# A two-layer hybrid decoder trunk on one core: new order of the first stage, its first transfers, the clears of the gated attention's tiles, and one operation at the end

## The chip, the cores and the metric

The kernel runs on one core of a Trainium2 chip. Its time is the device time of one execution in microseconds (us); the runs of a kernel give a median. A profile is of one execution, and has a time of its own. Engines: PE is TensorE (the matrix products), DVE is VectorE, ACT is ScalarE, POOL is GpSimd, SP is SyncE, which here only issues DMAs.

## What is computed

Two layers over x of 1024 tokens by 1024, in float32. The start of each layer, which the change is about, and its end:

```
c_act = silu(c)
mod = c_act @ w_mod + b_mod                      # 1024 -> 3*1024
shift, scale, gate = split(mod)
h = rms_norm(x, pre_gain) * (1.0 + scale) + shift
proj = h @ w_in                                  # to the heads of A, B, C and their gates
...
y = concat([a_out, r_out, g_out]) @ w_out
x = x + gate * rms_norm(y, post_gain)
```

A is sliding-window attention with rotary positions, B retention, C gated linear attention; each is multiplied by the silu of its own part of proj (gg is C's gate, rg B's, ga the low-rank input of C's decay).

## The kernel before, in words

Every float32 product is made of three passes of a faster format: an operand is split into a high part (a copy that rounds) and a low part (what the copy left, by a subtraction), and PE adds high by high, high by low and low by high. So each weight and each piece of h costs a copy (`high`, or line 503 for weights, mostly on ACT) and a subtraction (lines 844, 854 and 510, on DVE or POOL) before PE can use it. Weights come by DMA in pieces of 256 KB into staging tiles `st`.

The order of the work is written by the program itself while it is built: later stages are jobs, run when a running estimate of PE's time (`clk`) has passed their due time; a table `L` of lags shifts these due times. The first stage is not made of jobs. `first_stage` runs a list of steps written out by hand, `ORDER_1`, and its transfers are issued by another, `ORDER_0`, on SP's queue. The instructions of each engine stand in the order in which the steps emit them, and each engine works through its own list in order, waiting by semaphores for the others.

What the first stage computes: the modulation of layer 0 (shift and gain of 1024 columns) from eight pieces `wm` of w_mod, 1 MB each, and at the same time the norm and modulation of the first four token tiles (x0 to x3, 512 KB each), then from these the first product with gg's weights. The letters of `ORDER_1`, with their lines:

- `w`, `x`, `g`, `r`: issue a transfer (wm piece, x tile, a piece of gg's or rg's weights); `G`, `R`: split such a piece (lines 503 and 510); `v`: split ga's part (lines 865, 866).
- `q`, `o`, `n`: squares of an x tile on ACT (line 810), its root (line 618 on DVE, the power of line 621 on POOL), the scaling (line 816).
- `S`: the sum of a wm piece with c_act on PE (16 matmuls), copied by ACT (line 792); `C`: turn its row into columns (four small matmuls) and add the rows b_mod and norm gain (lines 798, 800), which PE had to transpose first.
- `T`, `U`: transposition of x tiles on PE, for tokens 0 to 255 and 256 to 511; `M`, `N`: modulation (line 829 on DVE, line 827 on ACT) and high part (line 835 on DVE, 833 on ACT); `L`, `K`: low part (lines 844, 854).
- `P`, `Q`: product of modulated pieces with gg's weights on PE (6 and 12 matmuls of 128x272).
- `t`: next step of the rotary table (VectorE operations of 512 columns in lines 372 to 398, one table load and two sines on ACT, lines 393 and 394).
- `z`, `y`: one spin, a product of the identity with itself whose result is never read. Number behind a letter: which piece, or how often.

`GLO` says which pieces of gg's (AG) and rg's (AV) first weights have the low part made on POOL. Ahead of the lists stand the transfers of c, constants (`c_early`), the positions, the rows b_mod and norm gain, and ga's weights, the positions' transposition, eight spins, and the silu of c (line 768's tanh on ACT, lines 770 and 771).

After the first stage the function `gla_tiles` (line 935) clears two tiles of 128x2048 for each layer, which C's products use as operands with zeros in places; the next projection of the heads follows. The layer's end (line 1595 on) computes the last two token tiles in halves; `rstd2` (line 624) adds two partial sums of squares (line 626), scales them and adds the epsilon (line 618), and takes the power -0.5 on POOL (line 621).

Of the kernel before, what the change touches and what calls it, by code (L numbers as in the profile page):

```python
# [91 lines left out]
def trunk(ctx: ExitStack, tc: tile.TileContext, ins, cst, out):  # L92
# [160 lines left out]
    c_nat = small(8)  # L253
    nc.sync.dma_start(c_nat, c_in.rearrange("o (p k) -> p (o k)", p=P))
    early = cload("early", eng=A)
# [368 lines left out]
    def rstd2(ss):  # L624
        sst = small(1)
        V.tensor_tensor(sst, ss[:, 0:1], ss[:, 1:2], ALU.add)
        return rstd_of(sst, 1, 1.0 / D, EPS)
# [93 lines left out]
    def first_stage():  # L721
# [3 lines left out]
        rows = t1()[0:24, 0:P]  # L725
        A.dma_start(rows[0:16, :], b_mod[0:1, 0:2 * D].rearrange("o (k p) -> (o k) p", p=P))
        A.dma_start(rows[16:24, :], pre_g[0:1, :].rearrange("o (k p) -> (o k) p", p=P))
        w = place(PLACE[0]["gg"])
        low = t1()[:, 0:128].rearrange("p (k n) -> p k n", k=KT)
        A.dma_start(low, w_ga[0])  # L730
        xk = [gp.tile([P, D], F32, tag=f"kT{t}", name=nm("xk"), bufs=1) for t in range(2)]
# [35 lines left out]
        V.tensor_copy(posf, pr[:, 0:8])  # L767
        A.activation(th0, c_nat, AF.Tanh, scale=0.5)
        more(3)
        V.scalar_tensor_tensor(c_act, th0, 1.0, c_nat, ALU.add, ALU.mult)  # L770
# [164 lines left out]
    def gla_tiles():  # L935

        for b in range(2):
            z_ = mix_tile(F32).rearrange("p a k q -> p (a k q)")
            G.memset(z_, 0.0)
# [574 lines left out]
    def last_output(l, load_mix):  # L1514
# [57 lines left out]
        for p in range(PLAIN // 2, NP_):  # L1572
# [52 lines left out]
            summed(y, pm, s1, s[:, 0:1], 0, h0)  # L1625
            V.tensor_tensor(s[:, 0:1], s[:, 0:1], s[:, 1:2], ALU.add)
            pm = bank()
            prod(pm[:, h1], a22, "T4", c=h1)
            add(y[:, h1], pm[:, h1], s1[:, h1])
            A.activation(stage()[:, h1], y[:, h1], AF.Square, accum_out=s[:, 2:3])  # L1630
            r = rstd2(s[:, 0:3:2])
            V.tensor_tensor(y[:, h1], y[:, h1], gcol[0][:, h1], ALU.mult)
# [207 lines left out]

ORDER_0 = "g x0 x1 w0 w1 x2 w2 g w3 g x3 w4 w5 w6"
ORDER_1 = (
# [4 lines left out]
)  # L1847
GLO = {'AG': (1, 3, 2), 'AV': (2,)}
B2, B1, BS, BST, MMB, SMB, BMOD = 10, 8, 11, 5, 2, 3, 3
# [56 lines left out]
}  # L1906
L = {"fx": 0.0, "fx@1": 3.24, "tt6": 12.28, "sw1": 2.01, "ld1": 1.66, "ld2": 1.76, "ld1@1": 0, "ld2@1": 0.07, "swW00": 5.37, "swT1": 0.43, "swW11": 1.72, "swW10": 6.15, "tt1": 15.57, "tt2": 5.14, "tt3": 7.18, "tt4": 3.16, "rq1": 17.87, "pf3@2": 0.68, "pf3@3": 1.67, "pf4@2": 4.07, "pf4@3": 9.27, "pf5": 0, "mod1": 12.02, "mod2": 2.2, "mod3": 8.51, "mod4": 8.54, "mod5": 4.17, "mod6": 9.91, "pre1": 9.84, "kv1": 4.07, "kv2": 9.26, "aq1": 6.02, "aq7": 6.16, "ag1": 4.54, "aq2": 2.75, "aq6": 6.49, "aq3": 11.06, "aq4": 6.85, "aq5": 4.05, "hn1": 8.92, "hn2": 6.14, "gz1": 18.33, "gz2": 11.8, "gl1": 9.81, "gd3": 17.03, "gc1": 0.98, "gc2": 6.16, "gc3": 1.97, "gc4": 0.1, "gc6": 0.8, "gc5": 1.44, "rc1": 3.56, "rc2": 2.88, "rc3": 7.08, "rc4": 5.77, "fin1": 8.69, "lay1": 0.27, "gc4@1": 0, "mod2@1": 4.09, "mod3@1": 12.43, "mod5@1": 4.25, "mod6@1": 5.5, "pre1@1": 7.09, "kv1@1": 5.87, "kv2@1": 2.64, "aq1@1": 4.88, "aq7@1": 5.14, "ag1@1": 2.87, "aq2@1": 1.05, "aq6@1": 6.78, "aq3@1": 8.64, "aq4@1": 5.48, "aq5@1": 5.73, "hn1@1": 8.28, "hn2@1": 0.73, "gz1@1": 15.9, "gz2@1": 11.94, "gl1@1": 3.31, "gd3@1": 16.2, "gc1@1": 0.0, "gc2@1": 2.01, "gc3@1": 0.83, "gc6@1": 1.61, "gc5@1": 0.72, "rc1@1": 4.88, "rc2@1": 2.79, "rc3@1": 5.12, "rc4@1": 0.8, "fin1@1": 8.37, "lay1@1": 11.61, "mod4@1": 5.36, "mod1@1": 6.02}
CHUNK = 7
# [44 lines left out]
```

## Time and profile before

| what | us |
|---|---|
| median of 3 runs | 967.53 |
| lowest and highest run | 965.69, 968.69 |
| the profiled execution's own time | 967.82 |
| its span, first to last instruction | 966.1 |
| PE busy | 949.9 (98%) |
| DVE, ACT, POOL busy | 670.2, 411.8, 238.9 |
| mean granted PE clock | 0.997 of full |
| DMA: read, written | 110.25 MB, 36.70 MB |

The span has 1.7 us less than the time. Busy time is no bound by itself: an engine's idle time costs something only where the engine that ends last waits for it. In the lists below a row has its start and its duration in us, the engine, the line of the kernel, the operation, what it writes and reads, how many such instructions follow each other, and in brackets how long the engine stood idle before and which instruction ended that. SPq and ACTq are the issues of DMAs.

### The profile page before, as it was taken

The numbers are of one execution on the slowest core, as the hardware profiler recorded it, in microseconds if no ns is written. First come the engines' busy times: TensorE is split into PE (matmuls) and PEld (weight loads), VectorE is DVE, ScalarE is ACT, GpSimd is POOL, SyncE is SP. The second block draws the span as 40 slices with busy tenths as digits, with TensorE's granted clock in tenths as the row PEclk, the third lists the DMA queues.
The fourth block names the chain that finished last, engine by engine and source line by source line (L and its number), as shares of the span: only waits on it lengthen the run. The fifth ranks groups of instructions, "written<-read, shape, count | busy, mean of one in ns | idle before, by whom it ended". The sixth has DMA issues, their size and how long they took to land.

```text
span 966.1 us, 17877 instructions
## 1 busy us (share of the span) xinstructions
PE 949.9 (98%) x6304; PEld 780.8 (81%) x6304; DVE 670.2 (69%) x1585; ACT 411.8 (43%) x1148; POOL 238.9 (25%) x309
## 2 busy tenths in 40 slices
PE   8899999999999999999999999999999999999996
PEld 6799888888888777778889988888888877777785
DVE  5886757767787977656667365775667668776885
ACT  3675601332323656624445462133234366754231
POOL 1431101213131424410024100122323124535000
PEclk9999999999999999999999999999999999999999
DMA  9756634414155456587545221442214434578883
GB/s 356 279 172 190 194 101 130 149 34 151 42 158 149 127 151 187 174 276 242 178 156 189 77 60 50 127 133 69 72 35 138 125 99 137 142 246 262 270 274 120
DMA packets 107527, 150.23 MB, mean 156 GB/s; under 512 B 11143, under 2 KB 58537, under 8 KB 106413
## 3 DMA queue, kind: packets, MB, share of 16 engines
q1 hardware_dynamic: 96140, 134.75, 44.7%
q10 hardware_dynamic: 11296, 14.34, 4.2%
q8 instruction: 50, 0.82, 0.4%
q14 instruction: 41, 0.33, 0.1%
HBM read 110.25 MB, written 36.70 MB: 152 GB/s over the span
## 4 chain that ended last, share of the span: by engine, by line
PE 90%; DMA 4%; DVE 3%; issue 1%; POOL 1%; ACT 1%; SPq 0%; DVEq 0%; POOLq 0%; ACTq 0%
PE mm L176 61%; PE aux L176 25%; PE aux L191 4%; DMA wm<-in_w_m_dram 2%; DMA st<-in_w_last_dram 1%; DMA t<-aoS 1%; POOL arena L540 0%; DVE t L1524 0%; DVE t L1529 0%; ACT st L1528 0%; DMA c_early<-cst_early_dram 0%; DVE t L1425 0%; DVE sincos L398 0%; PE mm L191 0%; DVE t L1758 0%
## 5 line engine op out<-in xcount | busy, mean ns | idle before, releaser
L176 PE MATMUL mm<-arena,arena 128*128 128x512 f32 (+2 forms) x1200 | 273.9, 379 | 0.0
L176 PE MATMUL mm<-arena 128*128 128x512 f32 (+2 forms) x1152 | 263.3, 381 | 0.0
L176 PEld LDWEIGHTS mm<-arena,arena 128*128 128x128 f32 x1200 | 205.1, 189 | 41.4 <-issue 2.9
L176 PEld LDWEIGHTS mm<-arena 128*128 128x128 f32 x1152 | 199.8, 189 | 40.5 <-issue 2.7
L621 POOL TENSOR_TENSOR sm<-sm,mhalf 128x1 f32<-128x1 f32 (+1 forms) x64 | 55.6, 868 | 298.7 <-DVE sm L618 179.6
L160 ACT ACTIVATE t<-aux 128x256 f32<-128x256 f32 (+2 forms) x124 | 51.9, 434 | 96.8 <-PE aux L191 73.2
L176 PE MATMUL mm<-arena,mx 128*128 128x512 f32 (+1 forms) x396 | 91.0, 384 | 0.9 <-ACT kept L1520 0.9
L176 PEld LDWEIGHTS mm<-arena,mx 128*128 128x128 f32 x396 | 70.4, 188 | 17.8 <-issue 1.9
L160 ACT ACTIVATE arena<-st 128x512 fp32r<-128x512 f32 x94 | 56.0, 626 | 40.0 <-PE mm L176 14.7
L510 POOL TENSOR_TENSOR arena<-st,arena 128x512 fp32r<-128x512 f32 x30 | 43.3, 1445 | 102.3 <-ACT arena L160 55.2
L1080 ACT ACTIVATE smx<-smx,sm 128x129 f32<-128x129 f32 x128 | 49.9, 393 | 38.4 <-DVE sm L1077 37.8
L510 DVE TENSOR_TENSOR arena<-st,arena 128x512 fp32r<-128x512 f32 x78 | 62.5, 824 | 2.6 <-ACT arena L160 0.9
L1084 POOL TENSOR_TENSOR smx<-smx,sm 128x512 f32<-128x512 f32 x32 | 35.5, 1109 | 112.6 <-DVE sm L1083 83.4
L176 PE MATMUL aux<-arena,mx 128*128 128x512 f32 x252 | 61.1, 397 | 0.0
L176 PEld LDWEIGHTS aux<-arena,mx 128*128 128x128 f32 x252 | 47.2, 188 | 11.4 <-issue 0.4
L327 DVE SCALAR_TENSOR_TENSOR acc<-ms,c_act,acc 128x512 f32<-128x512 f32 x60 | 46.4, 774 | 8.8 <-DMA ms<-in_w_mod_dram 7.6
L1128 ACT ACTIVATE t<-aux 128x256 f32<-128x256 f32 x32 | 12.2, 382 | 79.3 <-PE aux L176 71.0
L176 PEld LDWEIGHTS aux<-t,mx 32*128 32x128 f32 (+1 forms) x896 | 39.7, 187 | 5.1 <-issue 2.3
L176 PE MATMUL aux<-t,mx 32*128 32x32 f32 (+1 forms) x896 | 40.7, 272 | 0.0
L1425 DVE SCALAR_TENSOR_TENSOR t<-t,sm,t 128x512 f32<-128x512 f32 x32 | 23.1, 749 | 18.4 <-DMA t<-in_x_dram 13.5
L1075 DVE COPY_PREDICATED smx<-c_masks,aux 128x256 f32<-128x256 int32 x64 | 25.3, 447 | 13.0 <-ACT smx L160 12.8
L1133 DVE TENSOR_TENSOR t<-aux,sm 128x256 f32<-128x256 f32 x32 | 13.6, 425 | 29.0 <-POOL sm L621 28.9
(271 smaller groups left out, 1524.7 us busy)
## 6 DMA issues: line engine op xcount, KB each, us to landing
st<-in_w_in_dram SPq DMA_DIRECT2D x96, 256.0 KB
ms<-in_w_mod_dram SPq DMA_DIRECT2D x64, 256.0 KB
mx<-mixS SPq DMA_DIRECT2D x20, 512.0 KB
st<-in_w_last_dram SPq DMA_DIRECT2D x36, 256.0 KB
wm<-in_w_m_dram SPq DMA_DIRECT2D x8, 1024.0 KB
mixS<-t SPq DMA_DIRECT2D x40, 128.0 KB
t<-in_x_dram SPq DMA_DIRECT2D x18, 256.0 KB
mixS<-t ACTq DMA_DIRECT2D x32, 128.0 KB
```

What stands on the lines that cost most here:

```text
L160: A.activation(dst, src, AF.Copy)
L176: T.matmul(dst, lhsT, rhs, start=start, stop=stop)
L191: T.transpose(dst, src, idn)
L327: V.scalar_tensor_tensor(acc, wt, c_act[:, k:k + 1], acc, ALU.mult, ALU.add)
L510: e.tensor_tensor(lo, st, f(hi), ALU.subtract)
L621: G.tensor_tensor(r, r, mhalf[:, :w], ALU.pow)
L1075: V.copy_predicated(sv, curmask.unsqueeze(1).to_broadcast((P, 2, P)), pv[:, :, n // P - 1, :])
L1080: A.activation(sm[:, h, :], sm[:, h, :], AF.Exp, bias=mx[:, h:h + 1], accum_out=sums[:, h:h + 1])
L1084: eng("pn").tensor_tensor(sm[:, :, 0:128], sm[:, :, 0:128], rs.unsqueeze(2).to_broadcast((P, 4, P)), ALU.mult)
L1128: A.activation(sq, po, AF.Square)
L1133: V.tensor_tensor(h4(g1), h4(po), r.unsqueeze(2).to_broadcast((P, 4, 64)), ALU.mult)
L1425: V.scalar_tensor_tensor(xt[j], yg[j], r, xt[j], ALU.mult, ALU.add)
```

## The change

Five edits, in the order of the program:

1. c is loaded by ACT's queue, in front of the constants, and no longer by SP's. The rows b_mod and norm gain and ga's weights are issued by ACT behind the tanh, and no longer in front of its table load.
2. `ORDER_0` issues x1 ahead of x0 and one more piece of gg ahead of w3, and the last piece of gg behind w6; `ORDER_1` is written anew; line 829's last piece (M7) is now made by ACT.
3. `GLO`: the low parts of all four pieces of gg are made by POOL, and another one of rg's.
4. `gla_tiles` clears by 512 columns on ACT, from a 128x1 zero, and no longer with one POOL memset for each tile. These copies are emitted where the clears were asked for by the program's order of jobs, in the middle of a layer.
5. At the end, the sum of two of the three squares is scaled and given the epsilon early (a `tensor_scalar`), and one `scalar_tensor_tensor` takes the place of the addition and the scaling behind the last square.

Four lags of `L` (pf3@2, pf3@3, pf4@2, pf4@3) change too; they set when x of the next tiles is loaded.

```diff
     c_nat = small(8)
-    nc.sync.dma_start(c_nat, c_in.rearrange("o (p k) -> p (o k)", p=P))
+    A.dma_start(c_nat, c_in.rearrange("o (p k) -> p (o k)", p=P))
...
         rows = t1()[0:24, 0:P]
-        A.dma_start(rows[0:16, :], b_mod[0:1, 0:2 * D].rearrange("o (k p) -> (o k) p", p=P))
-        A.dma_start(rows[16:24, :], pre_g[0:1, :].rearrange("o (k p) -> (o k) p", p=P))
         w = place(PLACE[0]["gg"])
         low = t1()[:, 0:128].rearrange("p (k n) -> p k n", k=KT)
-        A.dma_start(low, w_ga[0])
...
         A.activation(th0, c_nat, AF.Tanh, scale=0.5)
+        A.dma_start(rows[0:16, :], b_mod[0:1, 0:2 * D].rearrange("o (k p) -> (o k) p", p=P))
+        A.dma_start(rows[16:24, :], pre_g[0:1, :].rearrange("o (k p) -> (o k) p", p=P))
+        A.dma_start(low, w_ga[0])
...
     def gla_tiles():
+        zero = small(1)
+        V.memset(zero, 0.0)
         for b in range(2):
             z_ = mix_tile(F32).rearrange("p a k q -> p (a k q)")
-            G.memset(z_, 0.0)
+            for c in range(0, 2 * KT * P, 512):
+                A.activation(z_[:, c:c + 512], zero.to_broadcast((P, 512)), AF.Copy)
...
             V.tensor_tensor(s[:, 0:1], s[:, 0:1], s[:, 1:2], ALU.add)
+            V.tensor_scalar(s[:, 0:1], s[:, 0:1], 1.0 / D, EPS, ALU.mult, ALU.add)
...
             A.activation(stage()[:, h1], y[:, h1], AF.Square, accum_out=s[:, 2:3])
-            r = rstd2(s[:, 0:3:2])
+            r = rstd_of(s[:, 2:3], 1, 1.0 / D, s[:, 0:1])
...
-ORDER_0 = "g x0 x1 w0 w1 x2 w2 g w3 g x3 w4 w5 w6"
+ORDER_0 = "g x1 x0 w0 w1 x2 w2 g g w3 x3 w4 w5 w6 g"
...
-    "q1 g q0 t1 w7 o1 o0 n1 n0 v t1 G z9 S0 r z1 h r z2 T0 T2 t2 z1 C0 S1 M0V z3 q2 z1 L0 P0 C1 M1A S2 "
...
-    "G C7 N2AAA t1 K2 U3 N3VVA t3 M7V L7 K3 t1 R R Q1 Q2 P6 P7 R t1 R Q3 t2 "
+    "q0 z1 t1 z1 y1 z1 v z1 y2 z1 q1 w7 z1 o0 z1 o1 y1 z2 y1 n0 y2 z1 y1 z3 n1 S0 z1 T0 t1 T2 z1 h G "
...
+    "C5 T3 M5V S6 L5 U1 y1 N1AAA P5 G C6 U2 K0 S7 t1 a M6V L6 K1 N2AAV t1 K2 Q0 C7 U3 M7A Q1 N3VVA r "
+    "L7 K3 R t1 P6 Q2 t4 R R P7 Q3 t1 R t1 "
 )
-GLO = {'AG': (1, 3, 2), 'AV': (2,)}
+GLO = {'AG': (3, 1, 0, 2), 'AV': (0,)}
```

Three places where instructions move. First ACT's list at the start of the program, before (DMA rows are issues; `t_6` holds the rows, `t_7` ga's weights, `sm_72` is c, `xk` an x tile):

```order
L250 DMA c_early<-cst_early_dram 128x192
L258 DMA posi<-in_positions_dram 8x128
L726 DMA t_6_98<-in_b_mod_dram 16x128
L727 DMA t_6_98<-in_pre_norm_gain_dram 8x128
L730 DMA t_7_101<-in_w_ga_dram 128x128
L768 ACT_TABLE_LOAD
L768 ACTIVATE sm_79<-sm_72 128x8
L810 ACTIVATE wm,sm_160<-xk_104 128x1024
```

and now:

```order
L254 DMA sm_72<-in_c_dram 128x8
L250 DMA c_early<-cst_early_dram 128x192
L258 DMA posi<-in_positions_dram 8x128
L765 ACT_TABLE_LOAD
L765 ACTIVATE sm_79<-sm_72 128x8
L766 DMA t_6_98<-in_b_mod_dram 16x128
L767 DMA t_6_98<-in_pre_norm_gain_dram 8x128
L768 DMA t_7_99<-in_w_ga_dram 128x128
L810 ACTIVATE wm,sm_162<-xk_100 128x1024
```

The three issues have moved behind the tanh, and c's issue has come to the front.

Second, PE's list from the eight spins to the first sum S0, before (`aux<-c_early` is a spin, `x8` eight of them; `mm<-c_early,t_6` is the transposition of the rows; `aux<-wm,c_act` is S0, and its rows' 8 are pairs):

```order
L176 MATMUL aux_127<-c_early 128x128 x8
L191 MATMUL mm_151<-c_early,t_6_98 128x24
L176 MATMUL aux_127<-c_early 128x128 x9
L176 MATMUL aux_128<-wm,c_act 32x256 x8
L176 MATMUL aux_127<-c_early 128x128 x3
```

and now, from the transposition on:

```order
L191 MATMUL mm_153<-c_early,t_6_98 128x24
L176 MATMUL aux_126<-c_early 128x128 x2
L176 MATMUL aux_161<-c_early 128x128
L176 MATMUL aux_126<-c_early 128x128 x2
L176 MATMUL aux_161<-c_early 128x128 x2
L176 MATMUL aux_126<-c_early 128x128 x3
L176 MATMUL aux_161<-c_early 128x128
L176 MATMUL aux_126<-c_early 128x128 x2
L176 MATMUL aux_161<-c_early 128x128 x3
L176 MATMUL aux_126<-c_early 128x128
L176 MATMUL aux_161<-c_early 128x128
L176 MATMUL aux_126<-c_early 128x128 x3
```

21 spins stand where there were 9, of both kinds (`z` into `aux_126`, `y` into `aux_161`), and S0 follows them.

Third, DVE's list at the end of the stage, before (lines 396 and 398 are the table's, `sincos`; lines 829, 835 and 844 make the modulated piece M7 and its low part; line 854 is the low part of two pieces):

```order
L798 SCALAR_TENSOR_TENSOR mod_5_97<-aux_159,sm_154,sm_153 128x1
L800 TENSOR_TENSOR mod_4_96<-aux_159,sm_153 128x1
L854 TENSOR_TENSOR arena_71<-t_63_479,arena_71 128x2x256
L829 TENSOR_SCALAR t_65_491<-mm_486,mod_5_97,mod_4_96 128x256 x2
L396 SCALAR_TENSOR_TENSOR sincos<-sincos 128x8x64
L398 TENSOR_SCALAR sincos<-sincos 128x8x64
L829 TENSOR_SCALAR t_66_497<-mm_388,mod_5_97,mod_4_96 128x256
L835 CAST arena_71<-t_66_497 128x256
L844 TENSOR_TENSOR arena_71<-t_66_497,arena_71 128x256
L854 TENSOR_TENSOR arena_71<-t_65_491,arena_71 128x2x256
```

and now:

```order
L835 CAST arena_71<-t_62_477 128x2x256
L854 TENSOR_TENSOR arena_71<-t_62_477,arena_71 128x2x256
L798 SCALAR_TENSOR_TENSOR mod_5_97<-aux_161,sm_156,sm_155 128x1
L800 TENSOR_TENSOR mod_4_96<-aux_161,sm_155 128x1
L829 TENSOR_SCALAR t_65_520<-mm_500,mod_5_97,mod_4_96 128x256 x2
L844 TENSOR_TENSOR arena_71<-t_64_505,arena_71 128x256
L854 TENSOR_TENSOR arena_71<-t_65_520,arena_71 128x2x256
L396 SCALAR_TENSOR_TENSOR sincos<-sincos 128x8x64
L398 TENSOR_SCALAR sincos<-sincos 128x8x64
```

The table's two steps have moved behind the last modulated pieces, and M7's line 829 and 835 are gone from DVE (ACT makes them, `t_64`).

More of the change, by code (lines that the diff above doesn't have):

```diff
@@ L1906 @@
 }
-L = {"fx": 0.0, "fx@1": 3.24, "tt6": 12.28, "sw1": 2.01, "ld1": 1.66, "ld2": 1.76, "ld1@1": 0, "ld2@1": 0.07, "swW00": 5.37, "swT1": 0.43, "swW11": 1.72, "swW10": 6.15, "tt1": 15.57, "tt2": 5.14, "tt3": 7.18, "tt4": 3.16, "rq1": 17.87, "pf3@2": 0.68, "pf3@3": 1.67, "pf4@2": 4.07, "pf4@3": 9.27, "pf5": 0, "mod1": 12.02, "mod2": 2.2, "mod3": 8.51, "mod4": 8.54, "mod5": 4.17, "mod6": 9.91, "pre1": 9.84, "kv1": 4.07, "kv2": 9.26, "aq1": 6.02, "aq7": 6.16, "ag1": 4.54, "aq2": 2.75, "aq6": 6.49, "aq3": 11.06, "aq4": 6.85, "aq5": 4.05, "hn1": 8.92, "hn2": 6.14, "gz1": 18.33, "gz2": 11.8, "gl1": 9.81, "gd3": 17.03, "gc1": 0.98, "gc2": 6.16, "gc3": 1.97, "gc4": 0.1, "gc6": 0.8, "gc5": 1.44, "rc1": 3.56, "rc2": 2.88, "rc3": 7.08, "rc4": 5.77, "fin1": 8.69, "lay1": 0.27, "gc4@1": 0, "mod2@1": 4.09, "mod3@1": 12.43, "mod5@1": 4.25, "mod6@1": 5.5, "pre1@1": 7.09, "kv1@1": 5.87, "kv2@1": 2.64, "aq1@1": 4.88, "aq7@1": 5.14, "ag1@1": 2.87, "aq2@1": 1.05, "aq6@1": 6.78, "aq3@1": 8.64, "aq4@1": 5.48, "aq5@1": 5.73, "hn1@1": 8.28, "hn2@1": 0.73, "gz1@1": 15.9, "gz2@1": 11.94, "gl1@1": 3.31, "gd3@1": 16.2, "gc1@1": 0.0, "gc2@1": 2.01, "gc3@1": 0.83, "gc6@1": 1.61, "gc5@1": 0.72, "rc1@1": 4.88, "rc2@1": 2.79, "rc3@1": 5.12, "rc4@1": 0.8, "fin1@1": 8.37, "lay1@1": 11.61, "mod4@1": 5.36, "mod1@1": 6.02}
@@ new lines @@
+L = {"fx": 0.0, "fx@1": 3.24, "tt6": 12.28, "sw1": 2.01, "ld1": 1.66, "ld2": 1.76, "ld1@1": 0, "ld2@1": 0.07, "swW00": 5.37, "swT1": 0.43, "swW11": 1.72, "swW10": 6.15, "tt1": 15.57, "tt2": 5.14, "tt3": 7.18, "tt4": 3.16, "rq1": 17.87, "pf3@2": 1.85, "pf3@3": 2.84, "pf4@2": 3.18, "pf4@3": 6.8, "pf5": 0, "mod1": 12.02, "mod2": 2.2, "mod3": 8.51, "mod4": 8.54, "mod5": 4.17, "mod6": 9.91, "pre1": 9.84, "kv1": 4.07, "kv2": 9.26, "aq1": 6.02, "aq7": 6.16, "ag1": 4.54, "aq2": 2.75, "aq6": 6.49, "aq3": 11.06, "aq4": 6.85, "aq5": 4.05, "hn1": 8.92, "hn2": 6.14, "gz1": 18.33, "gz2": 11.8, "gl1": 9.81, "gd3": 17.03, "gc1": 0.98, "gc2": 6.16, "gc3": 1.97, "gc4": 0.1, "gc6": 0.8, "gc5": 1.44, "rc1": 3.56, "rc2": 2.88, "rc3": 7.08, "rc4": 5.77, "fin1": 8.69, "lay1": 0.27, "gc4@1": 0, "mod2@1": 4.09, "mod3@1": 12.43, "mod5@1": 4.25, "mod6@1": 5.5, "pre1@1": 7.09, "kv1@1": 5.87, "kv2@1": 2.64, "aq1@1": 4.88, "aq7@1": 5.14, "ag1@1": 2.87, "aq2@1": 1.05, "aq6@1": 6.78, "aq3@1": 8.64, "aq4@1": 5.48, "aq5@1": 5.73, "hn1@1": 8.28, "hn2@1": 0.73, "gz1@1": 15.9, "gz2@1": 11.94, "gl1@1": 3.31, "gd3@1": 16.2, "gc1@1": 0.0, "gc2@1": 2.01, "gc3@1": 0.83, "gc6@1": 1.61, "gc5@1": 0.72, "rc1@1": 4.88, "rc2@1": 2.79, "rc3@1": 5.12, "rc4@1": 0.8, "fin1@1": 8.37, "lay1@1": 11.61, "mod4@1": 5.36, "mod1@1": 6.02}
```

4 rows, old and new, of the table ORDER_1 are left out of this document.

## The prediction

> **What bounds the kernel now.** I read the waits of TensorE (PE) first, then its timeline up to the first projection, then the stretches and the other engines around the one long wait, then the queues, and last the end of the run. The waits of PE (us in total, times, longest):
>
> ```profile
> PE mm L191 <- DVE posr L763: 3.3, 1, 3.3
> PE aux L176 <- DVE arena L835: 2.2, 1, 2.2
> PE aux L176 <- DMA wm<-in_w_m_dram: 2.1, 3, 1.0
> PE mm L176 <- ACT kept L1520: 0.9, 1, 0.9
> ```
>
> These are all: 8.5 us of a span of 966.1, and all but the last (0.9, near the end) lie in the first stage. Outside it, only PE's own work, which the change leaves alone, or the tail after its last matmul can give time. So the question is when the first projection starts. PE's timeline (start, duration, line, group; a pair of `c_early` matmuls is one spin, an empty product that keeps PE's clock up):
>
> ```profile
> 3.49 3.78 PE L176 MATMUL aux<-c_early 128*128 128x128 f32 x16
> 7.20 0.30 PE L191 MATMUL mm<-c_early,t 24*128 24x24 f32 x1
> 7.43 2.51 PE L176 MATMUL aux<-c_early 128*128 128x128 f32 x18
> 10.47 1.07 PE L176 MATMUL aux<-wm,c_act 128*32 128x256 f32 x16 [0.53 <-DMA wm<-in_w_m_dram]
> ...
> 18.50 1.50 PE L176 MATMUL aux<-c_early 128*128 128x128 f32 x12
> 19.84 0.51 PE L176 MATMUL aux<-sm,t 128*128 128x1 f32 x4
> ...
> 35.16 1.07 PE L176 MATMUL aux<-wm,c_act 128*32 128x256 f32 x16
> ...
> 38.90 3.99 PE L176 MATMUL aux<-arena 128*128 128x272 f32 x30
> 45.06 4.05 PE L176 MATMUL aux<-arena 128*128 128x272 f32 x18 [2.18 <-DVE arena L835]
> 48.95 1.23 PE L176 MATMUL mm<-arena,arena 128*128 128x256 f32 x9
> ```
>
> The row at 7.20 is the transposition of the rows (b_mod and the norm gain); the first `wm` row is the first modulation sum S0 (10.47), the row at 35.16 the last, S7; 48.95 is the first projection. One stretch of the stage and two behind the 2.18 us gap (length, busy time of PE, PEld, DVE, ACT and POOL, then PEclk):
>
> ```profile
> 20.00:30.00 10.00, 8.42 (x89) 6.55 (x91) 5.20 (x17) 3.61 (x8) 2.87 (x4) 1.00 1.02 421
> ...
> 46.00:47.00 1.00, 1.00 (x6) 1.00 (x6) 1.00 (x3) 0.66 (x2) 0.43 (x1) 0.50 0.00 0
> ...
> 48.00:49.00 1.00, 1.00 (x7) 1.00 (x6) 0.42 (x1) 0.29 (x3) 0.43 (x2) 0.54 0.00 0
> ```
>
> The gap costs twice: behind it the granted clock is 0.50 until shortly before 49. The 18 matmuls then take 48.95-45.06 = 3.89 us; the 30 before the gap took 45.06-2.18-38.90 = 3.98, 0.133 each, so 18 are worth 2.39. The half clock costs 1.50, the gap 2.18. What fills the gap (VectorE, DVE, and GpSimd, POOL):
>
> ```profile
> 36.16 0.29 DVE L835 CAST arena<-t 128x256 fp32r<-128x256 f32 x1
> ...
> 41.30 1.81 POOL L939 MEMSET mx<- 128x2048 f32 x1 [0.28 <-DMA c_late<-cst_late_dram]
> 41.48 1.91 DVE L398 TENSOR_SCALAR sincos<-sincos 128x512 f32<-128x512 f32 x1
> ...
> 43.60 1.26 POOL L510 TENSOR_TENSOR arena<-st,arena 128x512 fp32r<-128x512 f32 x1
> 43.87 1.14 DVE L835 CAST arena<-t 128x256 fp32r<-128x256 f32 x1
> ```
>
> Line 398 ends as the memset ends (43.39 against 43.11), line 835 as POOL's line 510 ends (45.01 against 44.86), and line 835 takes 1.14 where it took 0.29 with POOL idle: both are held up by the POOL operation beside them. PE waits for the second.
>
> **The change part by part.** The sum is made against the profiled execution, 967.82 us (span 966.1 and 1.7 around it), which lies 0.29 above the median of 967.53; that is inside the runs' own spread (965.69 to 968.69), so I correct nothing.
>
> *Transfers of the start.* The rows' DMAs go behind the table load and the tanh on ACT, and c comes ahead of them. ACT's rows, and VectorE's first:
>
> ```profile
> 0.80 0.39 SPq L254 DMA_DIRECT2D sm<-in_c_dram  x1
> ...
> 1.24 0.58 ACTq L258 DMA_DIRECT2D posi<-in_positions_dram  x1
> 1.85 0.32 ACTq L726 DMA_DIRECT2D t<-in_b_mod_dram  x1
> 2.21 0.34 ACTq L727 DMA_DIRECT2D t<-in_pre_norm_gain_dram  x1
> ...
> 2.96 1.28 ACT L768 ACT_TABLE_LOAD   x1 [2.96 <-issue]
> 3.02 0.21 DVE L763 CAST posr<-posi 8x128 f32<-8x128 int32 x1 [2.09 <-DMA posi<-in_positions_dram]
> ...
> 4.25 0.21 ACT L768 ACTIVATE sm<-sm 128x8 f32<-128x8 f32 x1
> ```
>
> One issue of 0.4 us ahead moves the positions, `posr` and the first eight spins 0.4 later: they end at 7.6 instead of 7.20. On ACT three issues (to 2.25), the load (1.28) and the tanh (0.21) end near 3.75; b_mod is issued at 3.8 and the gain at 4.1. How long the gain takes to land isn't in a row: at most 7.20-2.21 = 4.99 us, and the positions, issued while nothing else moved, took 1.78. So the rows land between 5.9 and 9.1, and the transposition stands between 7.6 (the spins' end) and 9.1. I take 4.4 us, nearer the loaded end, since SyncE's queue (SP) is as full as it was then: 8.5, a wait of 0.9. SP loses the issue of c (0.39 us), so its whole stream starts 0.4 earlier; one more weight piece of 256 KB then stands ahead of the fourth `wm` piece, and as many ahead of the last as before.
>
> In the first 40 us the queues were (packets, MB):
>
> ```profile
> q1 hardware_dynamic: 3936, 14.26, 92.1%
> q10 hardware_dynamic: 352, 0.18, 1.6%
> ```
>
> ACT's five requests of that time (96, 64, 8, 4 and 4 KB) add up to q10's 0.18 MB: the rows have a queue of their own. The Trainium skill ("DMA: Bandwidth & Descriptors", Queues, rings and completion order) says that each DMA engine takes turns between queues, a packet at a time; by that rule the rows wait for a few packets and not for the bytes that SP has queued, and the late issue costs what the issue is late. The trace agrees as far as it goes; no row here shows rows issued behind a queued `wm` piece.
>
> *More spins, PE's sum.* Between the transposition and S0 there are 21 spins in place of 9, in the whole stage 8 more (x16 records). A spin costs (19.84-18.50)/6 = 0.22 warm, 2.51/9 = 0.28 at the start: 8 cost 1.8 to 2.2, I take 2.0. From the transposition to the first projection PE took 48.95-7.20 = 41.75; without its waits for `wm` (2.1), the gap (2.18) and the half clock (1.50) that is 35.97, with the spins 38.0. With the transposition at 8.5 the first projection starts at 46.5, **2.45 us earlier** (7.6 gives 45.6, 9.1 gives 47.1: 1.85 to 3.35).
>
> This holds if the `wm` pieces come in time. S0 stands near 8.5+0.3+21x0.25 = 14, 3.5 later than before, so the first pieces, which PE waited for by 0.5 to 1.0, are early; the last sum is near 46.5-9.8 = 36.7, while its piece was there at 35.16.
>
> *The table steps and the memset.* Behind S7's start the PE work is 1.0 for the sum, 60 matmuls (48 of the before and a group of 12 that stood ahead) by 0.133, and two small groups of some 0.4: 9.8 us. DVE and ACT rows of before for the steps that now follow S7:
>
> ```profile
> 37.09 1.01 ACT L827 ACTIVATE t<-mm,mod,mod 128x256 f32<-128x256 f32 x2
> ...
> 40.09 0.63 ACT L393 ACTIVATE sincos<-mx 128x512 f32<-128x512 f32 x1
> ...
> 41.67 2.17 ACT L503 ACTIVATE arena<-st 128x512 fp32r<-128x512 f32 x4
> ...
> 43.31 0.53 DVE L829 TENSOR_SCALAR t<-mm,mod,mod 128x256 f32<-128x256 f32 x1
> ...
> 45.38 0.69 DVE L854 TENSOR_TENSOR arena<-t,arena 128x512 fp32r<-128x512 f32 x1
> ```
>
> The last coefficients are there near S7+3.2 (the sum, the 12 matmuls and a small group). Behind them DVE now does two line 829 (1.06), a subtraction no longer than line 854 and line 854 (1.4 together), and only then the table: the last piece is ready near S7+5.7 and needed by the last 12 matmuls, near S7+8.2. That is covered by 2.5, of which one POOL operation (1.26) could take half. Next late is ACT: from S7+1.0 a copy of S7's sum (0.4), three line 827 (1.5), the table load that stood ahead (1.28), two sines (1.26), two line 833 (a sine's length each at most) and four line 503 (2.17) make 7.9, to S7+8.9, where the first projection needs its weights at S7+9.8. Cover 0.9; if it fails, PE waits by what is missing. So the gap and the half clock go, and nothing of the same size is next. The swapped places of the first two x pieces, the later lags of x loads and the four low parts of the gate weights that are POOL's now (one more of 1.26) I cost at nothing: POOL is busy 2.87 of the 10 us from 20, and what it can hold up on DVE is the 1.26 just counted.
>
> *Clears on ACT.* POOL's memsets (1.81 each) go. Per layer ACT gets eight copies of 512 columns. By line 503's row (2.17 for four) one costs 0.54, eight 4.3. In layer 0 they stand between 169 and 185, where ACT is busy 5.99 of 16 us (below):
>
> ```profile
> 169.00:185.00 16.00, 16.00 (x96) 13.33 (x97) 13.44 (x36) 5.99 (x14) 4.09 (x4) 1.00 0.47 150
> ```
>
> PE waits for ACT in neither layer's middle, so the likely price is nothing; the other bound is a queue of four copies, 2.2, in front of something that PE needs, and in both layers 4.4. I take 0.2 in all, by the rows' side.
>
> *The end.* The last rows:
>
> ```profile
> 960.12 0.16 DVE L626 TENSOR_TENSOR sm<-sm 128x1 f32<-128x1 f32 x1
> 960.20 0.42 DVE L1632 TENSOR_TENSOR t<-t,modg 128x256 f32<-128x256 f32 x1
> 960.53 0.15 DVE L618 TENSOR_SCALAR sm<-sm 128x1 f32<-128x1 f32 x1
> ```
>
> Line 618 stood behind line 1632 on DVE. One operation now takes the place of lines 626 and 618, and stands at 626's: the power on POOL can start at 960.28 for 960.68, 0.4 earlier, and what follows it with it. The lower bound is one operation, 0.15; I take 0.4.
>
> Sum: 967.82-2.45-0.4+0.2 = 965.2.
>
> **The rivals.** *Everything comes off:* the rows land by 7.6, so no wait and no cold clock. The first projection at 45.6 and nothing for the clears: 967.82-3.35-0.4 = 964.1. For it: the queue of their own; against: 4.99 is a bound that was measured under less load.
>
> *The cold clock is moved, not removed:* the wait for the rows opens a gap on PE at 7.6. Waits up to 1.0 left the clock at 1.00 (two of the three for `wm` lie in 20 to 30), one of 2.18 halved it, so somewhere between a landing of 8.6 and 9.8 it halves for some 3.4 us, among spins at first, and costs about what it cost there, 1.5. Then the first projection is at 9.3+38+1.5 = 48.8 and the total 967.5. For it: nothing fills that gap. The Trainium skill ("TensorE: Matmul & The Clock Gate", the table of clock states) has the clock fall after an idle window of 3.4 us; by that no wait expected here would cost a clock, but by it the 2.18 us gap wouldn't have either, and the rows at 46 show 0.50: the measurement decides.
>
> *Slower:* the rows land behind the `wm` pieces that SP queued before their issue. The pieces came 3.5 us apart at most ((35.16-10.47)/7), so the second was there by 14. If the rows land with it, at 13, PE idles 5.4 us from 7.6, runs at half clock behind that (1.5), and the first projection is at 13+38+1.5 = 52.5: 3.55 later, 967.82+3.55-0.4+0.2 = 971.2. It decides from a landing of about 12.4 on (slower by 2.9 with the end's gain taken off). Against: q10 is not q1.
>
> *It doesn't do what it says:* `wm` alone bounds the stage. Then S7 can't move before 34.8 (0.4 earlier), but S7+9.8 = 44.6 is ahead of my 46.5, so this would take a slower stream, of 2 us or more: 967.
>
> **How the numbers follow.** About 0.3%, 2.9 us, is what a measurement of this kernel can tell from no change, so the bound of faster is about 964.7. Forecast (964.1 to 966.4, by transpositions from 7.6 to 9.1 and the small terms) 0.54; everything comes off 0.20; moved clock, a late stream or ACT's copies in the way (966.4 to 967.8) 0.20; slower 0.06. Faster: the second case and a third of the first, 0.38; same 0.56; slower 0.06. The range runs from 963.6, the second case with 0.5 for the runs' spread, to 967.6, which leaves out the slower case and the worst of the third.
>
> **What would show it.** Right: PE's waits without line 835, no 0.50 in PEclk after 12, the first projection between 45.6 and 47.1, S0 near 14 with no wait for `wm`, line 398 well under a microsecond, the power 0.4 sooner behind PE's end, no PE wait for ACT at 169 to 185. Wrong: a wait for `t` ahead of the transposition beyond 1.5 us, half clock behind it, a PE wait for ACT's line 503 or 833 ahead of the projection, or time that moves in the middle of a layer, where I expect none.

## The result and the profile after

The changed kernel is **slower**: 968.93 us median of 18 runs against 965.97 of 18 runs of before, ratio 1.0032 with a 95% interval of 1.0024 to 1.0040. I had 965.2, faster by 0.27%, and a range that ends at 967.6. Of the runs of the kernels below, one execution of e1 took 4766.94 us and counts as slow; its figures are those of the other eleven.

The waits of TensorE (PE) in the changed kernel:

```profile
PE mm L191 <- DMA c_early<-cst_early_dram: 6.5, 1, 6.5
PE mm L176 <- ACT kept L1523: 1.6, 1, 1.6
```

The wait of 2.2 us for line 835 is gone, and those for the `wm` pieces too. In their place the first wait has doubled, from 3.3 to 6.5, and it is now one for the constants. PE's timeline, the rows that stand against those of before:

```profile
6.53 0.24 PE L191 MATMUL mm<-c_early,posr 8*128 8x8 f32 x1 [6.53 <-DMA c_early<-cst_early_dram]
6.71 3.78 PE L176 MATMUL aux<-c_early 128*128 128x128 f32 x16
10.42 0.30 PE L191 MATMUL mm<-c_early,t 24*128 24x24 f32 x1
10.64 5.68 PE L176 MATMUL aux<-c_early 128*128 128x128 f32 x42
16.25 1.07 PE L176 MATMUL aux<-wm,c_act 128*32 128x256 f32 x16
...
40.78 1.07 PE L176 MATMUL aux<-wm,c_act 128*32 128x256 f32 x16
...
44.15 6.26 PE L176 MATMUL aux<-arena 128*128 128x272 f32 x48
50.26 4.96 PE L176 MATMUL mm<-arena,arena 128*128 128x256 f32 x40
```

From 6.53 on PE never stops in this stage: the 48 last matmuls come in one piece, in 6.1 us. But everything hangs on the start. The transposition of the rows is at 10.42 for 7.20, S0 at 16.25 for 10.47, the first projection at 50.26 for 48.95. Where the start goes (SyncE's and ScalarE's issues, then the waits for what they bring):

```profile
0.80 0.41 ACTq L254 DMA_DIRECT2D sm<-in_c_dram  x1
...
0.80 0.39 SPq L165 DMA_DIRECT2D st<-in_w_in_dram  x1
...
1.25 0.90 SPq L738 DMA_DIRECT2D xk<-in_x_dram  x2
1.25 0.45 ACTq L250 DMA_DIRECT2D c_early<-cst_early_dram  x1
...
1.72 0.58 ACTq L258 DMA_DIRECT2D posi<-in_positions_dram  x1
...
4.72 0.21 ACT L765 ACTIVATE sm<-sm 128x8 f32<-128x8 f32 x1 [1.10 <-DMA sm<-in_c_dram]
4.73 0.32 ACTq L766 DMA_DIRECT2D t<-in_b_mod_dram  x1
...
6.10 0.22 DVE L760 CAST posr<-posi 8x128 f32<-8x128 int32 x1 [5.16 <-DMA posi<-in_positions_dram]
```

ScalarE's three first requests are 4, 96 and 4 KB, and each is waited for until some 4 to 5 us behind its issue: c until 4.72 (3.9 us), the constants until 6.53 (5.3), the positions until 6.10 (4.4). Before, the positions took 1.78 and PE could start at 3.29. Two things differ: SyncE's 256 KB piece is issued at 0.80 and not behind c at 1.24, and the constants are issued 0.45 later; e9 below tells the two apart.

The end, from PE's last 24 matmuls, before and then changed:

```profile
955.58 2.99 PE L176 MATMUL mm<-arena,a 128*128 128x256 f32 x24
...
960.82 0.92 POOL L621 TENSOR_TENSOR sm<-sm,mhalf 128x1 f32<-128x1 f32 x1 [2.26 <-DVE sm L618]
961.78 1.41 DVE L1425 SCALAR_TENSOR_TENSOR t<-t,sm,t 128x512 f32<-128x512 f32 x2 [0.44 <-POOL sm L621]
```

```profile
957.72 2.99 PE L176 MATMUL mm<-arena,a 128*128 128x256 f32 x24
...
962.56 0.60 POOL L621 TENSOR_TENSOR sm<-sm,mhalf 128x1 f32<-128x1 f32 x1 [1.86 <-DVE sm L620]
962.67 2.07 DVE L1428 SCALAR_TENSOR_TENSOR t<-t,sm,t 128x512 f32<-128x512 f32 x3
```

From the first of these to the end of the last line 1428 it takes 962.67+2.07-957.72 = 7.02 us; before it was 961.78+1.41-955.58 = 7.61.

The two profiled executions differ by 1.6 us (967.82 and 969.42): 1.31 at the first projection, 0.59 won at the end, and between the projection and the last 24 matmuls 0.83 (906.63 before, 907.46 now), of which 0.7 is the longer wait for line 1520, 1523 now. So little else moved in the layers' middle. The medians differ by 2.96. The rest lies in the execution of before that I had read: a second profile of the same kernel (below, `e4_before_again`) has its first projection at 46.58 and not at 48.95. Against that one the change loses 3.7 us in the first stage and wins 0.6 at the end: 3.1, without the wait for line 1523.

### The profile page after: what moved, and what is told of

Its sections match the earlier page's. It is cut to its first block, busy times and chain, and to the rows that moved or that the text cites. A ratio compares the mean times of both kernels' runs of the same rounds, so it can differ in the third digit from the quotient of the medians.

```text
span 967.7 us, 17959 instructions
## 1 busy us (share of the span) xinstructions
PE 952.5 (98%) x6336; PEld 782.6 (81%) x6336; DVE 668.6 (69%) x1589; ACT 417.4 (43%) x1161; POOL 235.0 (24%) x306
## 5 line engine op out<-in xcount | busy, mean ns | idle before, releaser
L510 POOL TENSOR_TENSOR arena<-st,arena 128x512 fp32r<-128x512 f32 x31 | 45.6, 1472 | 107.3 <-ACT arena L160 63.9
L1083 ACT ACTIVATE smx<-smx,sm 128x129 f32<-128x129 f32 x128 | 49.9, 392 | 39.6 <-DVE sm L1080 39.0
```

Of the source, the lines that this page charges most:

```text
L510: e.tensor_tensor(lo, st, f(hi), ALU.subtract)
L1083: A.activation(sm[:, h, :], sm[:, h, :], AF.Exp, bias=mx[:, h:h + 1], accum_out=sums[:, h:h + 1])
```

## The experiments

Eleven kernels, each timed against the kernel before on its own chip (three chips, medians of before from 966.17 to 966.41, so medians of different rows are good to some tenths). "Rows" is the start of the rows' transposition, "projection" that of the first projection, in the profiled execution; "gap" is the longest wait of PE from the first eight spins to there.

| kernel | rows | projection | gap | median us | ratio to before, interval |
|---|---|---|---|---|---|
| before, first profile | 7.20 | 48.95 | 2.18, half clock | 965.97 | |
| changed | 10.42 | 50.26 | none | 968.93 | 1.0032 (1.0024 to 1.0040) |
| e1, c on SyncE again | 8.95 | 49.66 | 1.77 ahead of the rows, half clock | 968.55 | 1.0024 (1.0011 to 1.0037) |
| e2, 9 spins | 10.76 | 47.82 | none | 966.47 | 1.0016 (1.0003 to 1.0030) |
| e3, before, new start | 10.62 | 48.49 | 2.16 | 967.95 | 1.0021 (1.0012 to 1.0029) |
| e4, before again | 7.22 | 46.58 | 2.03 | 965.73 | 0.9997 (0.9988 to 1.0006) |
| e5, changed, old start | 7.23 | 47.39 | none | 965.29 | 0.9989 (0.9979 to 1.0000) |
| e6, the same, 9 spins | 6.84 | 45.56 | 1.28 ahead of S0 | 964.54 | 0.9983 (0.9968 to 0.9998) |
| e7, before, clears on ScalarE | 7.17 | 44.16 | 0.4 | 963.34 | 0.9975 (0.9966 to 0.9984) |
| e8, before, new end | 7.22 | 46.48 | 2.13 | 965.95 | 0.9993 (0.9983 to 1.0003) |
| e9, constants ahead of c | 11.87 | 52.55 | 1.82 ahead of the rows, half clock | 971.24 | 1.0050 (1.0036 to 1.0064) |
| e10, changed, memsets back | 10.27 | 49.35 | none | 968.47 | 1.0027 (1.0018 to 1.0036) |
| e11, before, clears and end | 7.22 | 44.49 | 0.8 | 962.96 | 0.9966 (0.9954 to 0.9977) |

**e1: c on SyncE's queue again**, in the changed kernel.

```diff
-    A.dma_start(c_nat, c_in.rearrange("o (p k) -> p (o k)", p=P))
+    nc.sync.dma_start(c_nat, c_in.rearrange("o (p k) -> p (o k)", p=P))
```

> The changed kernel with c loaded by SyncE's queue again, so that the constants are ScalarE's first transfer; all else as changed. Theory 1 (the start is lost because the constants are issued 0.45 us later, when SyncE's weight and x transfers are already moving, and land at 6.4 for 2.84): the constants land near 2.9, TensorE's first transposition is back near 3.3, the rows are issued near 3.6 and land by 8.7, their transposition stands at 7.2 to 9 for 10.42, and the first projection comes 1.4 to 3.2 us earlier: 965.7 to 967.5 for 968.9. Rival (the start doesn't matter, the time is lost in the layers, by ScalarE's clears): the median stays within 0.5 of 968.9.

The waits of PE:

```profile
PE mm L191 <- DVE posr L760: 3.3, 1, 3.3
PE mm L191 <- DMA t<-in_pre_norm_gain_dram: 1.8, 1, 1.8
```

The start is back at 3.3: it was the place of c that cost it. But the first projection came only 0.6 earlier, since now the rows are late, and PE stands 1.77 us in front of them. What that does is in the stretches behind (PE busy first, PEclk behind POOL):

```profile
7.00:10.37 3.37, 1.60 (x14) 1.39 (x13) 1.01 (x4) 1.15 (x2) 0.00 (x0) 1.00 1.02 418
10.38:13.79 3.41, 3.41 (x19) 3.41 (x18) 1.11 (x4) 1.35 (x3) 1.07 (x2) 0.50 1.02 419
```

Half clock for 3.41 us. This is the rival of the moved clock, in a kernel that undoes half of the first edit.

**e2: 9 spins for 21** between the rows and S0, the rest as changed.

```diff
-    "q0 z1 t1 z1 y1 z1 v z1 y2 z1 q1 w7 z1 o0 z1 o1 y1 z2 y1 n0 y2 z1 y1 z3 n1 S0 z1 T0 t1 T2 z1 h G "
+    "q0 t1 z1 y1 v z1 y1 q1 w7 z1 o0 o1 y1 z1 n0 y1 z1 n1 S0 z1 T0 t1 T2 z1 h G "
```

> The changed kernel with 9 spins for 21 between the rows' transposition and the first sum, as before; the start as changed. Theory 2 (TensorE bounds the first stage now, and the change adds 16 spins and not the 8 of the prediction): 12 spins by 0.27 go, 3.2 us, the first sum is at 13.0 for 16.25 and the first projection near 47 for 50.26, about 965.7. Rival (the stage is bound by the w_mod pieces or by the x tiles, the spins only fill waits): the first sum comes earlier, a wait of the same length opens behind it, the first projection moves by less than 1 us.

```profile
10.76 0.30 PE L191 MATMUL mm<-c_early,t 24*128 24x24 f32 x1
13.80 1.07 PE L176 MATMUL aux<-wm,c_act 128*32 128x256 f32 x16
47.82 4.36 PE L176 MATMUL mm<-arena,arena 128*128 128x256 f32 x35
```

From the rows to the projection it takes 37.06 for 39.84: 2.8 us for 12 spins, 0.23 each, and no new wait of PE in the stage. PE does bound it, and every spin costs its time.

**e3: the first edit alone**, in the kernel before.

```diff
-    nc.sync.dma_start(c_nat, c_in.rearrange("o (p k) -> p (o k)", p=P))
+    A.dma_start(c_nat, c_in.rearrange("o (p k) -> p (o k)", p=P))
...
-        A.dma_start(rows[0:16, :], b_mod[0:1, 0:2 * D].rearrange("o (k p) -> (o k) p", p=P))
-        A.dma_start(rows[16:24, :], pre_g[0:1, :].rearrange("o (k p) -> (o k) p", p=P))
...
-        A.dma_start(low, w_ga[0])
...
         A.activation(th0, c_nat, AF.Tanh, scale=0.5)
+        A.dma_start(rows[0:16, :], b_mod[0:1, 0:2 * D].rearrange("o (k p) -> (o k) p", p=P))
+        A.dma_start(rows[16:24, :], pre_g[0:1, :].rearrange("o (k p) -> (o k) p", p=P))
+        A.dma_start(low, w_ga[0])
```

> The kernel before with the first edit alone: c in front on ScalarE's queue, the rows and ga's weights behind the tanh. Theory 1: the constants land near 6.4, the rows' transposition stands near 10.4 for 7.2; 2.1 us of waits for w_mod pieces take up part of the 3.2, the rest, about 1.1 us, is lost: 967.1 for 966.0. If nothing takes it up, 969.2. Rival (the start doesn't matter): within 0.3 of 966.0.

```profile
10.62 0.30 PE L191 MATMUL mm<-c_early,t 24*128 24x24 f32 x1
48.49 3.75 PE L176 MATMUL mm<-arena,arena 128*128 128x256 f32 x30
```

2.0 us lost by the ratio, 1.9 by the projection (48.49 against 46.58 in e4). The rows stand 3.4 later, and PE no longer waits for a `wm` piece: these waits took up part of it, as the theory had it, though in e4 they are only 0.9 to begin with. Another 0.4 came back because the nine spins behind the rows took 2.49 for the 2.90 of e4. The edit is a loss by itself.

**e4: the kernel before, unchanged.**

> The kernel before, unchanged, for another profile of it. Theory 3 (the profiled execution of the prediction was a slow one of its kind, 967.8 against a median of 966.0 in 18 runs, since the half clock behind the 2.18 us gap comes in some executions only): the gap is there, the clock behind it is 1.00 and the first projection is near 47.4, or it is 0.50 again with a time near 967.8. Rival (the half clock always comes, and the spread is elsewhere): 0.50 with a time near 966.

```profile
44.21 2.54 PE L176 MATMUL aux<-arena 128*128 128x272 f32 x18 [2.03 <-DVE arena L835]
46.58 5.68 PE L176 MATMUL mm<-arena,arena 128*128 128x256 f32 x46
```

The gap is the same, but the 18 matmuls behind it take 2.37 and not 3.89. No half clock. So the 1.50 belongs to some executions. What decides it can be read from stretches of 3.41 us. Before, in its first profile; then e9; then e3, whose gap is as long as the first one's:

```profile
42.09:45.50 3.41, 1.23 (x10) 1.02 (x9) 3.34 (x5) 1.75 (x4) 2.77 (x3) 1.00 0.11 36
45.50:48.91 3.41, 3.41 (x17) 3.41 (x16) 2.82 (x5) 1.92 (x4) 1.75 (x4) 0.50 0.03 8
```

```profile
9.60:12.98 3.38, 1.56 (x13) 1.34 (x13) 1.30 (x5) 0.00 (x0) 0.00 (x0) 1.00 1.01 410
13.00:16.40 3.40, 3.40 (x18) 3.40 (x18) 1.39 (x5) 1.35 (x3) 1.40 (x2) 0.50 1.01 408
```

```profile
42.04:45.45 3.41, 1.94 (x16) 1.72 (x14) 3.34 (x4) 2.87 (x6) 3.15 (x4) 1.00 0.00 1
45.45:48.86 3.41, 2.72 (x22) 2.72 (x23) 3.38 (x6) 1.71 (x3) 1.48 (x3) 1.00 0.06 17
```

In the three falls of this stage (before, e9, e1) the gap lies whole in the 3.41 us ahead, and PE was busy there for 36%, 46% and 47%; then the clock is halved for 3.41. The borders come from the traces: in every one the time at full clock, by its clock records, is a whole number of 3.413 us (7.96 to 45.50 in the first profile of before, 11 times; 11.32 to 960.22 in e3, 278 times), as if windows of that length ran through. On these windows the gap of 2.16 in e3 is cut by a border, PE was busy for 57% and 80%, and nothing falls; the same holds for e4 (78% and 62%) and e8 (71% and 67%). Over all thirteen traces, the ends included, every such window behind the first rise with PE busy for 48% or less was followed by half clock, and none with 49.9% or more (49.9% is the window from 956.86 on in the first profile of before). So where the gap falls among the windows decides, and not its length alone. The Trainium skill ("TensorE: Matmul & The Clock Gate", Part 1) has a free-running window of 3413 ns; the length agrees with the traces. It asks for an idle window; here one that was busy for 47% was enough.

**e5 and e6: the first edit undone**, with 21 spins and with 9. The diff is e3's the other way round, and e6 has e2's too.

> The changed kernel with the whole first edit undone (c on SyncE's queue, the rows and ga's weights in front of the table load), the 21 spins kept. Theory 1 with the landings of the runs so far: the rows are there before the eight spins end, their transposition is back at 7.2 for 10.42 with no gap and no half clock (the run with c alone moved back had a gap of 1.77 there and half clock behind it); TensorE then needs 39.8 to the first projection as in the changed kernel: 47.0 for 50.26, 965.7 for 968.9. Rival (the w_mod pieces or the x tiles bound the stage then): waits for them open, the first projection stays behind 48.

> The changed kernel with the first edit undone and 9 spins for 21 ahead of the first sum: what the other edits of the first stage are worth alone. Theories 1 and 2 together: transposition at 7.2 and 37.1 from there (as in the run with 9 spins and the new start), 44.3 for 50.26, some waits for w_mod pieces of 0.3 to 1 us in all, no gap ahead of the last products: 963 to 964 for 968.9 and 966.0. Rival (the new order is worse in itself, by ScalarE's longer tail behind the last sum): a TensorE wait for ScalarE or VectorE of 1 to 2 us ahead of the first projection, 965 to 966.

```profile
7.23 0.30 PE L191 MATMUL mm<-c_early,t 24*128 24x24 f32 x1
47.39 4.84 PE L176 MATMUL mm<-arena,arena 128*128 128x256 f32 x39
```

With the rows' transposition back at 7.23 for 10.42, e5 wins 2.87 us at the projection. In the time it wins 3.6 by the two medians, 3.9 if each is set against before on its own chip (2.96 above it, 0.89 below it): the first edit costs the changed kernel about what it delays the start. e6 wins only 1.8 more at the projection, since part of the 12 spins covered something:

```profile
PE aux L176 <- DVE sm L618: 1.3, 1, 1.3
...
10.57 1.07 PE L176 MATMUL aux<-wm,c_act 128*32 128x256 f32 x16 [1.28 <-DVE sm L618]
```

S0 starts at 10.57 behind this wait, and at 10.5 to 10.8 in every kernel with the old start and 9 spins (e4, e7, e8, e11), where the row names the first `wm` piece. S0 reads that piece and `c_act` and nothing of line 618. By the completions recorded in the trace the piece landed at 10.43, 0.14 ahead of S0; in the first profile of before it landed at 10.34, 0.13 ahead. So the piece is the cause here too, and the name in the row is not. The expected 44.3 was missed by 1.3: from the rows, which came at 6.84, to the projection it took 38.72 for 37.06, by this wait and two of 0.2 to 0.3. e6 beats before, just; e5 lies at the edge of its interval.

**e7: the clears on ScalarE alone**, in the kernel before.

```diff
+        zero = small(1)
+        V.memset(zero, 0.0)
...
-            G.memset(z_, 0.0)
+            for c in range(0, 2 * KT * P, 512):
+                A.activation(z_[:, c:c + 512], zero.to_broadcast((P, 512)), AF.Copy)
```

> The kernel before with the clears on ScalarE alone. Theory 4 (GpSimd's memsets hold up line 398 by 1.5 us and so make most of the gap of 2.0 to 2.2 us; in the layers ScalarE's copies are hidden): line 398 takes 0.43 to 0.7 for 1.91, the gap shrinks to 0.5 to 1.3 and no clock falls behind it, the first projection near 45.5, 964.5 to 965 for 966.0. Rival A (GpSimd's low part just starts earlier and holds up other VectorE operations instead): the gap stays above 1.5, no change. Rival B (the copies delay something TensorE needs at 170 to 180 or 640 to 680): a TensorE wait there, and 966.5 or more.

```profile
37.96 6.36 PE L176 MATMUL aux<-arena 128*128 128x272 f32 x48
...
40.54 0.43 DVE L398 TENSOR_SCALAR sincos<-sincos 128x512 f32<-128x512 f32 x1
...
41.45 0.29 DVE L835 CAST arena<-t 128x256 fp32r<-128x256 f32 x1
...
42.47 1.50 POOL L510 TENSOR_TENSOR arena<-st,arena 128x512 fp32r<-128x512 f32 x1 [4.53 <-ACT arena L503]
...
44.16 5.92 PE L176 MATMUL mm<-arena,arena 128*128 128x256 f32 x48
```

Line 398 takes 0.43 for 1.91 and line 835 0.29 for 1.14, and the gap is gone altogether, not only smaller: line 835 is now done before GpSimd's next low part starts, which had held it up before. 2.8 us by the medians, from one edit of three lines, and PE has no wait between 100 and 800 us, where the copies stand.

**e8: the new end alone**, in the kernel before.

> The kernel before with the fifth edit alone. From the two profiles: the power on GpSimd stood 5.24 us behind the start of TensorE's last 24 matmuls before and 4.84 in the changed kernel, and took 0.92 and 0.60: from that row to the last VectorE operation's end 0.5 to 0.7 us go. 965.4 for 966.0, hardly to be told from no change in the median; the profile's tail shows it. Rival (nothing, the output's transfers end last): the time from TensorE's end to the end of the span stays at 7.5.

```profile
957.62 0.60 POOL L621 TENSOR_TENSOR sm<-sm,mhalf 128x1 f32<-128x1 f32 x1 [1.86 <-DVE sm L620]
957.73 2.07 DVE L1425 SCALAR_TENSOR_TENSOR t<-t,sm,t 128x512 f32<-128x512 f32 x3
```

The power takes 0.60 for 0.92, and the three last operations run on in one piece. With PE's last 24 matmuls from 952.76 on, the tail is 7.04 for 7.61. The median can't tell 0.6 (0.9993, the interval holds 1).

**e9: the constants ahead of c**, both on ScalarE's queue, in the changed kernel.

```diff
-    A.dma_start(c_nat, c_in.rearrange("o (p k) -> p (o k)", p=P))
     early = cload("early", eng=A)
+    A.dma_start(c_nat, c_in.rearrange("o (p k) -> p (o k)", p=P))
```

> The changed kernel with the constants in front of c on ScalarE's queue (both stay there): the constants are issued at 0.80 as before, but SyncE's first weight piece of 256 KB at 0.80 too, for 1.24 before. Theory A (the constants share the DMA engines with whatever SyncE has issued at the same time): they land near 4.7, as c's 4 KB did in that place; c lands near 6, the rows are issued then and land past 10, so a gap of 1 to 2 us opens ahead of their transposition and the first projection is no earlier than 49.5: 968 to 970. Theory B (only their own late issue counts): they land near 2.9, the start is back near 3.3, and c alone is late; the rows bound the transposition, again near 10.

```profile
6.38 0.27 PE L191 MATMUL mm<-c_early,posr 8*128 8x8 f32 x1 [6.38 <-DVE posr L760]
...
11.87 0.24 PE L191 MATMUL mm<-c_early,t 24*128 24x24 f32 x1 [1.82 <-DMA t<-in_pre_norm_gain_dram]
```

```profile
6.94 0.21 ACT L765 ACTIVATE sm<-sm 128x8 f32<-128x8 f32 x1 [3.32 <-DMA sm<-in_c_dram]
```

The constants are issued at 0.80 as in e1, and SyncE's first weight piece at 0.80 and not at 1.25: the start is at 6.38 and not at 3.28. The row names the positions as the last to come; by the completions recorded in the trace the constants landed at 5.29, for 2.84 before and 6.40 in the changed kernel. c, issued second, was there at 6.94, 5.7 us later. So it is less the 0.45 us of a later issue than SyncE's stream beside it (theory A). The DMA packets say the same. Until 2.6 us ScalarE's queue (q10) had moved 160 packets and 0.10 MB before, all of the constants and positions, beside 0.04 MB on SyncE's (q1), whose weight piece came only behind c. In e9 it had moved 32 packets and 0.02 MB beside 53 and 0.11 MB of q1; in the changed kernel 61 small packets, less than 0.005 MB, beside 83 and 0.17 MB. Where both queues have work, the packets of both go through side by side. The rows, which wait for the tanh, are late in turn: a gap, half clock, and the slowest kernel of all.

**e10: the memsets on GpSimd again**, in the changed kernel (e7's diff the other way round).

> The changed kernel with the clears on GpSimd again, all else as changed. In the kernel before, moving them was worth 2.8 us, since the memset held up line 398, which stood in front of the last modulated piece. Theory (in the new order the table's steps stand behind the last pieces, so that nothing TensorE needs is behind them): line 396 or 398 takes 1.8 or more again, TensorE waits 0 to 0.5 us more, 968.9 to 969.4. Rival (the memset still holds up a subtraction that TensorE waits for): a gap of 1 us or more ahead of the last products or the first projection, 970 or more.

```profile
45.56 1.82 POOL L939 MEMSET mx<- 128x2048 f32 x1
...
47.56 1.40 DVE L398 TENSOR_SCALAR sincos<-sincos 128x512 f32<-128x512 f32 x1
```

No loss: 968.47, as the changed kernel within the intervals. With the table's steps behind the last modulated pieces, the memset holds up nothing that PE waits for. The clears (e7) and the new order (here, with the other edits) cure the same gap; either is enough. That its projection is 0.9 ahead of the changed kernel's has another reason: its 21 spins take 5.06 us from the rows to S0 (10.27 to 15.33), for 5.83. A spin costs 0.47 in the changed kernel's first eight (3.78) and 0.22 later, and when PE's clock rises differs from run to run: the traces record the first full clock from 9.92 on in e10 and from 12.20 on in the changed kernel.

**e11: clears and end together**, in the kernel before.

> The kernel before with the fourth and fifth edits alone (clears on ScalarE, one operation less at the end): a version meant to beat both. The clears gave 963.3 for 966.2, the end 0.55 us from the start of TensorE's last 24 matmuls to the end of the last VectorE operation (9.69 before, 9.14 in the changed kernel by their rows): 962.8. If the two do not add, 963.3.

962.96, a ratio of 0.9966: faster than both kernels. Two figures in the expectation (9.69 and 9.14) came from rows that don't belong together; the rows give 7.61 and 7.02, 0.59 apart for the 0.55 there. The new order adds nothing to this: e6, which has edits 2 to 5 with 9 spins, has its projection at 45.56, 1.07 behind e11's 44.49. It still has four spins more in the stage (34 for 30), which are worth 0.9.

## Why the prediction was wrong

*"One issue of 0.4 us ahead moves the positions, `posr` and the first eight spins 0.4 later: they end at 7.6 instead of 7.20."* This step failed, and with it the sign. I costed the moved request by its issue (0.4) and moved the landings along unchanged. But c had held SyncE's stream back by one issue while the constants and positions passed, and without it their packets move among that stream's. The spins ended at 10.42: 2.8 us past the 7.6. Shown by e3 (the edit alone costs 2.0 in the kernel before), e1, e9 and their packets. The 1.78 us in which the positions came "while nothing else moved" was thus a figure with c in front of the stream, and no figure for the changed kernel, where they took 4.4. The rule of turns between queues of the Trainium skill ("DMA: Bandwidth & Descriptors", Queues, rings and completion order) I had weighed for the rows alone: by the same rule the constants take turns with a 256 KB piece and two x tiles, and I hadn't asked that of the first requests. The packets of e9 agree with it (32 beside 53 until 2.6); the price, a landing at 5.29 for 2.84, is a measurement of these runs. That the rows' landing at 8.5 would bound the transposition was wrong as well: c came at 4.72, the rows were issued at 4.73, and they were there before the late spins ended.

*"8 more (x16 records)."* Wrong by a factor of two. There are 30 spins in the old order and 46 in the new; PE's list counts spins and the profile's rows two records for each, and I took the difference of 16 in the list for records. 16 by 0.22 are 3.5 us in place of 2.0. From the rows to the projection I had 38.0, measured are 39.84. The two steps together are the projection's miss: 1.9 (10.42 for 8.5) and 1.8 make 3.7, of 46.5 to 50.26.

*The base.* The sum took a gap of 2.18 and a half clock of 1.50 from one execution. The gap is in all four profiles with the old order and the memsets (2.03 to 2.18), the half clock in one of four. So, if these four stand for the runs, in most of them 1.5 of the gain was not there to be won; the median of 18 is 1.85 below the execution that I read, and the sum says "I correct nothing".

*What held.* The gap and its cause: with line 398 not behind a memset it goes (e7). The cover of the tail behind S7: no wait of PE for ScalarE or VectorE in the changed kernel, 9.48 from S7 to the projection where I had 9.8. The clears cost nothing in the layers. The end gave 0.59 for the 0.4 that I took. The `wm` pieces came in time.

*The rivals.* The moved clock came true in e1 and e9 and not in the changed kernel, whose spins, being late, cover the rows. The slower case came true by its sign, with another mechanism than mine (rows behind `wm` pieces): what was late was what PE needs for its very first instruction.

*Open.* The wait of PE for ACT's line 1520 near the end (1523 with the clears on ScalarE) is 0 to 1.7 us in these profiles (0.9 before, 1.6 changed, 0 in e2 and e3, 1.7 in e7). It is 0 to 0.9 in the five with the memsets and 0 to 1.7 in the eight with the copies, so a link with the fourth edit is neither shown nor excluded. And an order of its own for the old start, without the wait of e6, wasn't tried.

## What to carry to other kernels

Before moving a small early transfer to save its issue, list what the first instruction of the bounding engine needs, and ask what else will be on the DMA engines while it is on its way: here a request of 4 KB in front of the stream was worth 3 us as a gate (PE's start at 3.28 in e1 and at 6.38 in e9). When an engine goes from waiting to bounding, filler that was free becomes its full price, so count it in the program's own units. And take the base of a sum from more than one profile when a stall can trip a clock.

## What the runs showed of the hardware

- The constants (96 KB) and the positions (4 KB) on ScalarE's queue were there 2.0 and 1.8 us behind their issue where c stood ahead of SyncE's first 256 KB piece (before), and 5.3 and 4.4 us where that piece was issued at 0.80, with two 512 KB tiles behind it within a microsecond (changed). c's 4 KB, issued at 0.80 beside it, took 3.9. Constants issued at 0.80 in both landed at 2.84 (before) and 5.29 (e9).
- The clock fell behind a gap of 1.77 us (e1) and did not behind one of 2.16 (e3). Full clock lasted whole numbers of 3.413 us in all thirteen traces, and half clock 3.413 in the three falls of the first stage. Of the windows of that length, those with PE busy for 48% or less were followed by half clock, those with 49.9% or more not. One kernel can so differ by 1.5 us from run to run.
